# A convolutional feed-forward block's first pass: every sum on VectorE, two weight operands split at once, two pairs side by side

## The chip, the cores and the metric

The kernel runs on one core of a Trainium2 chip. The metric is the device time of one execution in microseconds, as the median over runs. Five engines work in order, each through its own queue, and wait for each other by semaphores: TensorE (PE in the profile; its weight loads are PEld), VectorE (DVE), ScalarE (ACT), GpSimd (POOL), and SyncE (SP), which here issues nearly all DMA transfers.

## The reference

One layer of a bidirectional encoder over 2304 positions (a request of 2048 and one of 256, with the same weights), model width 1024, feed-forward width 2816. The mixers come first (an mLSTM and a grouped attention); the change touches only what follows:

```
x = x + concat(m_out, a_out) @ w_out
h = rmsnorm(x, norm2_w)
u = centred_dwconv(h @ w_up, conv_w, conv_b)      # width 3 over positions
a, g = split(u, 2)                                # 2816 channels each
y = x + (silu(g) * a) @ w_down
out = rmsnorm(y, final_norm_w)
```

All data are float32.

## The kernel before

**Stages.** The program runs the input projection and the mixers, then the output projection with the second norm (`phase_c`, lines 893 to 975, matmuls at L932), then the **first pass** of the feed-forward (`up_phase`: `h @ w_up`, convolution, gate), then the second pass (`down_phase`, matmuls at L1311). Before the code of the first pass is reached, `body` begins it inside `phase_c`: it forms the first block's operand sums, loads three operands and starts one pair.

**Seven products for eight.** A product with operands cut 2 by 2 is done with seven block products and some sums of blocks. Positions are cut in three blocks `b` of 772, 768 and 764 columns, each in two halves of 386, 384 and 382. Seven stationary-side operands come from `w_up` and seven moving ones from `h`; they are named `11`, `21`, `22` (blocks as they are) and `t1` to `t4` (sums). Float32 operands are split in a high part, rounded to fp32r by ScalarE (L1050 for weights, L1007 for `h`), and the rest, by a VectorE subtraction (L1051, L1008); each product takes three matmuls (hi·hi, hi·lo, lo·hi) for each of 4 chunks of 128, so 12 matmuls in a row.

**A pair** is two neighbouring rows of 128 channels (`jj`, `jj + 1`) of `w_up`; it takes the seven products, 84 matmuls, into three PSUM banks `pa`, `pb`, `pc`. Between products ScalarE copies `pa` or `pc` out to tiles `u` (L1101) and VectorE adds (L1104); `pa` and `pc` go on accumulating after such a copy, so the next product into the bank waits for it. Each **turn** `gi` (0 to 10) of a block has two pairs, the gate's and then the value's. The pairs' PSUM tiles lie by turns in two pools of four banks. In `up_start` a pair loads its weights (`ru`), does products `11` and `21`; in block 0 its four weight sums are formed on GpSimd (`w_sums`, L1039) and stored to DRAM (`wsu_d`), from where blocks 1 and 2 load them; the returned `rest` does the other five.

**After a pair.** `conv` does the centre tap on ScalarE (L1173) and two taps on VectorE (L1180, 768 columns each); `silu` is on ScalarE; VectorE multiplies gate and value (L1223); GpSimd forms the sums for the second pass (L1196); all is stored to `act_d`. Turns 3 to 6 of blocks 0 and 1 also form the next block's operand sums on GpSimd (`n2_sums`, L1027), and every turn of block 1 forms sums of `w_down` (`w_sums` again) for the second pass. `n2_block` loads and splits the next block's seven operands.

**What sets the order.** The code is written to the queues by a scheduler that lays out the instructions of each engine ahead of time from its own times; tile pools with a number of buffers (`RW` for raw weights, `WU` for split ones, `UB` for `u`, `TMB` for sums) decide which load has to wait for which release. On the chip each queue is followed strictly in that order.

Of the kernel before, what the change touches and what calls it, by code (L numbers as in the profile page):

```python
# [37 lines left out]
NB = T // BT  # L38
NTB = 8
CX = 8  # L40
WU = 6
NX0 = 2
NPC = 1
WSTEP = 2
# [20 lines left out]
LEAD = 1.3  # L65
WD = 4
YB = 4
UB = 3
RW = 5
PO = 4  # L70
PB = 4
PEB = 3
# [959 lines left out]
def w_sums(g, s1, a11, a12, a21, a22, dst, nm):  # L1032


    nc = g.nc
    t1, t2, t4 = (s1.tile([P, D // 2], F32, tag="tmp", name=f"tw{k}_{nm}", bufs=TMB) for k in (1, 2, 4))
    for k, o, p, q, op in ((2, t1, a21, a22, ALU.add), (0, t2, t1, a11, ALU.subtract),
                           (1, a21, a11, a21, ALU.subtract), (3, t4, a12, t2, ALU.subtract)):
        nc.gpsimd.tensor_tensor(o, p, q, op)  # L1039
        g.st.dma_start(dst[:, k], o)  # L1040
    return {"t1": t1, "t2": t2, "t3": a21, "22": t4}


def split_w(g, s1, src, nm):


    nc = g.nc
    w = s1.tile([P, 2, NCC // 2, P], F32R, tag="wu", name="wu" + nm, bufs=WU)
    hi, lo = (w[:, a].rearrange("p c n -> p (c n)") for a in range(2))
    nc.scalar.activation(hi, src, AF.Copy)  # L1050
    nc.vector.tensor_tensor(lo, src, f32(hi), ALU.subtract)  # L1051
    return w


def up_start(g, s1, ps, ops, b, jj):


    nc = g.nc
    n = (DT[b + 1] - DT[b]) // 2
    nm = f"{b}_{jj}"  # L1060
    h = D // 2

    def raw(k):
        return s1.tile([P, D], F32, tag="raw", name=f"ru{k}_{nm}", bufs=RW)
    r1, r2 = raw(1), raw(2)
    nc.sync.dma_start(r1, g.w_up[jj].rearrange("p c n -> p (c n)"))
    wsrc = {"11": r1[:, 0:h], "21": r1[:, h:D], "t4": r2[:, h:D]}
    dst = g.wsu_d[jj // 2]
    if b:
        r3, r4 = raw(3), s1.tile([P, h], F32, tag="tmp", name=f"ru4_{nm}", bufs=TMB)  # L1070
        nc.sync.dma_start(r3, dst[:, 0:2].rearrange("p k n -> p (k n)"))
        nc.sync.dma_start(r2[:, 0:h], dst[:, 2])
        nc.sync.dma_start(r4, dst[:, 3])
        nc.sync.dma_start(r2[:, h:D], g.w_up[jj + 1, :, NCC // 2:NCC].rearrange("p c n -> p (c n)"))
        wsrc.update({"t2": r3[:, 0:h], "t3": r3[:, h:D], "t1": r2[:, 0:h], "22": r4})
    else:
        nc.sync.dma_start(r2, g.w_up[jj + 1].rearrange("p c n -> p (c n)"))

    def bank(k):
        return ps.tile([P, 512], F32, tag="p", name=f"p{k}_{nm}", bufs=PB)[:, 0:n]  # L1080

    def mul(p, k, add=False):

        w = split_w(g, s1, wsrc[k], f"{k}_{nm}")
        for c in range(NCC // 2):
            for i, (aa, bb) in enumerate(((0, 0), (0, 1), (1, 0))):
                nc.tensor.matmul(p, w[:, aa, c, :], ops[k][:, c, bb, 0:n], start=c == 0 and i == 0 and not add,  # L1087
                                 stop=c == NCC // 2 - 1 and i == 2, skip_group_check=add)
    p1, p2 = bank("a"), bank("b")
    mul(p1, "11")  # L1090
    mul(p2, "21")
    if not b:
        wsrc.update(w_sums(g, s1, r1[:, 0:h], r1[:, h:D], r2[:, 0:h], r2[:, h:D], dst, nm))

    def rest(u1, u2):


        u11, u12, u21, u22 = u1[:, 0:n], u1[:, n:2 * n], u2[:, 0:n], u2[:, n:2 * n]

        def copy(o, p):  # L1100
            nc.scalar.activation(o, p, AF.Copy)  # L1101

        def add(o, p, q):
            nc.vector.tensor_tensor(o, p, q, ALU.add)  # L1104
        copy(u11, p1)
        add(u11, p2, u11)
        mul(p1, "t2", True)
        copy(u12, p1)
        p3 = bank("c")
        mul(p3, "t1")  # L1110
        copy(u21, p3)
        mul(p1, "t3", True)
        copy(u22, p1)
        add(u22, u22, u21)
        mul(p3, "22", True)
        add(u12, p3, u12)
        mul(p1, "t4", True)
        copy(u21, p1)
    return rest


def n2_block(g, s1, sl, sa, b):
    ops = {}
    for k, e in zip(OPS, P1):
        ops.update(n2_ops(sa if b == 1 and k in TWICE else s1 if k in EARLY else sl, b, [k]))
        n2_load(g, ops, b, k, engs=e)
    return ops

# [12 lines left out]
def up_phase(g, tc, st, s1, sl, banks, ops, first):  # L1141
# [10 lines left out]
    nc.sync.dma_start(cw, g.conv)  # L1152
    NC = NW - BLK
    carry = sa.tile([P, 2 * NFC, NC], F32, name="carry")
    turn = [0]
    H = BLK // 2

    def up(b, j):

        rest = first.pop() if first else up_start(g, s1, banks[turn[0] % 2], ops, b, j)  # L1160
        turn[0] += 1
        us = [sp.tile([P, NW], F32, tag="u", name=f"u{b}_{j + k}", bufs=UB) for k in range(2)]
        o = NC if b else 1
        nn = DT[b + 1] - DT[b]
        rest(*(u[:, o:o + nn] for u in us))
        return us

    def conv(b, jj, u, y):
# [18 lines left out]
    def act_ops(b, gi, ya):  # L1187
# [5 lines left out]
        b11, b12, b21, b22 = (ya[:, k, z] for k in range(2) for z in range(2))  # L1193
        t1, t2, t3, t4 = (ts[:, k] for k in range(4))
        for o, p, q in ((t1, b12, b11), (t2, b22, t1), (t3, b22, b12), (t4, b21, t2)):
            nc.gpsimd.tensor_tensor(o, p, q, ALU.subtract)  # L1196
        g.st.dma_start(g.act_d[b, 3:7, :, gi].rearrange("k p n -> p k n"), ts)

    for b in range(ND):
        if b:  # L1200
            ops = n2_block(g, s1, sl, sa, b)
        for gi in range(NG):
            j = 2 * gi
            if b < ND - 1 and SG <= gi < SG + NCC // 2:
                n2_sums(g, s1, b + 1, gi - SG)
            if b == 1:
                r = [s1.tile([P, D], F32, tag="raw", name=f"rd{gi}_{k}", bufs=RW) for k in range(2)]
                for k in range(2):
                    nc.sync.dma_start(r[k], g.w_down[0, (j + k) * P:(j + k + 1) * P, :])
                h = D // 2  # L1210
                w_sums(g, s1, r[0][:, 0:h], r[1][:, 0:h], r[0][:, h:D], r[1][:, h:D],
                       g.wsd_d[:, :, gi].rearrange("k p n -> p k n"), f"d{gi}")
            yg = sa.tile([P, 2, 2, H], F32, tag="y", name=f"yg{b}_{j}", bufs=YB)
            ya = sa.tile([P, 2, 2, H], F32, tag="y", name=f"ya{b}_{j}", bufs=YB)
            for y, jj in ((yg, j + NFC), (ya, j)):
                us = up(b, jj)
                for k in range(2):
                    yk = y[:, k].rearrange("p z n -> p (z n)")
                    conv(b, jj + k, us[k], yk)
                    if y is yg:  # L1220
                        nc.scalar.activation(yk, yk, AF.Silu)
                    else:
                        nc.vector.tensor_tensor(yk, yk, yg[:, k].rearrange("p z n -> p (z n)"), ALU.mult)  # L1223
            act_ops(b, gi, ya)


def down_phase(g, tc, st, s1, sl, banks):
# [23 lines left out]
    def wts(b, k, g0, g1):  # L1251
# [83 lines left out]
def body(tc, aps, phases="abcd"):  # L1335
# [5 lines left out]
    with ExitStack() as st:  # L1341
# [70 lines left out]
        with ExitStack() as s2:  # L1412
# [11 lines left out]
            for f in todo:  # L1424
                f()

            first = [up_start(g, s1, pd, ops, 0, NFC)]
            g.c_end()
            s_wo.close()
            phase_d(g, tc, s1, pd, ops, first)  # L1430
# [88 lines left out]
```

## Time and profile before

| | us |
|---|---|
| median of 3 runs | 3448.78 (3447.7 to 3454.29) |
| the profiled execution | 3458.05 |
| its span, first to last instruction | 3456.3 |
| outside the span | 1.75 |
| PE busy, share of the span | 95% |
| DVE busy | 77% |
| ACT busy | 59% |
| POOL busy | 35% |
| mean granted TensorE clock | 0.980 |

The first pass' matmuls begin at 1860 us and end at 2939 us of the span. A row of the groups view reads: line, engine, operation, output tile <- input tiles, shape, count; busy time and mean of one; the idle time of the engine just before, and what ended it. A row of the windows view has a stretch, its length, and then each engine's busy time with its count of instructions, the granted clock, the DMA engines' busy share and GB/s. Durations of neighbouring instructions overlap a little, and a matmul's duration is about twice the distance to the next start.

### The profile page before, as it was taken

Reading aid. Unit: us, or ns where it says so; the run is one execution under the profiler, and the core shown is the slowest. Engines: PE = TensorE matmul, PEld = TensorE weight load, DVE = VectorE, ACT = ScalarE, POOL = GpSimd, SP = SyncE. Lnnn points to the kernel's source line nnn. Section 1 sums busy time; section 2 is a strip of 40 time slices with the busy share of each in tenths; the row PEclk is TensorE's granted clock in tenths of the full one; section 3 lists DMA queues with packets and bytes.
Section 4 is the critical chain, followed back from the end, with each engine's and each line's share of the span. In section 5 each row is a group of like instructions: output and inputs, shape, how many; then the busy total and the mean of one; then the engine's idle time right before and its main releaser. Section 6 shows DMA issues by size and latency. Waiting matters only on the chain.

```text
span 3456.3 us, 56346 instructions
## 1 busy us (share of the span) xinstructions
PE 3299.8 (95%) x19566; PEld 3054.8 (88%) x19566; DVE 2650.3 (77%) x4298; ACT 2047.3 (59%) x4490; POOL 1205.7 (35%) x1370
## 2 busy tenths in 40 slices
PE   7989999999999999999997999998999999999998
PEld 6778888888888888878897989988999999999998
DVE  7875687778767787887754999998998888766664
ACT  4535666666666676665543645565567777655553
POOL 7774023213241332311136676655432111110101
PEclk9999999999999999999998999999999999999999
DMA  7765233233343434432258464577666556967673
GB/s 240 218 187 166 90 118 104 89 115 103 101 126 114 144 117 126 150 116 87 96 177 286 171 218 174 200 249 264 235 242 203 177 173 199 325 222 270 215 237 123
DMA packets 407085, 601.88 MB, mean 174 GB/s; under 512 B 32496, under 2 KB 256784, under 8 KB 406800
## 3 DMA queue, kind: packets, MB, share of 16 engines
q1 hardware_dynamic: 374256, 553.43, 48.8%
q0 software_dynamic: 11088, 33.04, 3.4%
q10 hardware_dynamic: 21456, 11.80, 1.1%
q8 instruction: 154, 2.52, 0.3%
q14 instruction: 131, 1.07, 0.1%
HBM read 434.23 MB, written 163.92 MB: 173 GB/s over the span
## 4 chain that ended last, share of the span: by engine, by line
PE 67%; DVE 11%; issue 7%; POOL 5%; ACT 5%; DMA 5%; SPq 0%; POOLq 0%; DVEq 0%; ACTq 0%
PE pa L1087 11%; PE pf L1311 7%; PE pc L1087 5%; PE po L932 4%; PE ph L1311 4%; PE mv L682 4%; PE mj L672 4%; PE ps L544 3%; PE pv L564 3%; PE ps L545 3%; PE pv L562 3%; PE pv L563 3%; PE px L521 3%; PE pb L1087 2%; PE pg L1311 2%
## 5 line engine op out<-in xcount | busy, mean ns | idle before, releaser
L550 DVE TENSOR_TENSOR xx<-pe,xx 128x512 fp32r<-128x512 f32 x520 | 371.7, 727 | 171.8 <-ACT xx L549 168.6
L1087 PE MATMUL pa<-nt,wut 128*128 128x386 f32 (+2 forms) x2376 | 457.4, 343 | 19.4 <-ACT u L1101 17.5
L1087 PEld LDWEIGHTS pa<-nt,wut 128*128 128x128 f32 x2376 | 427.2, 192 | 24.5 <-ACT u L1101 21.5
L548 ACT ACTIVATE pe<-ps 128x512 f32<-128x512 f32 x520 | 298.6, 595 | 155.6 <-PE ps L545 141.0
L522 DVE TENSOR_REDUCE mx<-px 128x1 f32<-128x512 f32 (+1 forms) x528 | 339.2, 670 | 50.8 <-PE px L521 49.7
L549 ACT ACTIVATE xx<-pe 128x512 fp32r<-128x512 f32 x520 | 316.1, 633 | 4.7
L932 PEld LDWEIGHTS po<-cmx,wo 128*128 128x128 f32 x1728 | 231.3, 190 | 17.9 <-DVE cx L937 0.8
L932 PE MATMUL po<-cmx,wo 128*128 128x256 f32 x1728 | 241.2, 282 | 0.9 <-DVE cx L937 0.6
L1196 POOL TENSOR_TENSOR ts<-ya 128x384 f32<-128x384 f32 x66 | 115.9, 1757 | 350.7 <-DVE ya L1223 347.4
L1051 DVE TENSOR_TENSOR wut<-ru,wut 128x512 fp32r<-128x512 f32 x220 | 224.9, 1023 | 16.9 <-ACT wut L1050 14.2
L564 PE MATMUL pv<-xx,vv 128*128 128x512 f32 x520 | 214.8, 413 | 13.0 <-DVE xx L550 12.8
L544 PE MATMUL ps<-qq,kk 128*128 128x512 f32 x520 | 214.6, 416 | 1.3 <-ACT pe L548 0.6
L562 PE MATMUL pv<-xx,vv 128*128 128x512 f32 x520 | 209.6, 403 | 1.9 <-ACT rs L572 1.1
L545 PE MATMUL ps<-qm,kl 65*128 65x512 f32 x520 | 208.5, 404 | 0.1
L563 PE MATMUL pv<-xx,vl 128*64 128x512 f32 x520 | 206.9, 398 | 0.0
L672 PE MATMUL mj<-mn,wm 128*128 128x256 f32 x1296 | 199.8, 288 | 6.7 <-ACT og L686 4.8
L682 PE MATMUL mv<-wm,mn 128*128 128x256 f32 x1296 | 204.0, 286 | 1.9 <-ACT qb L678 1.9
L672 PEld LDWEIGHTS mj<-mn,wm 128*128 128x128 f32 x1296 | 185.1, 193 | 22.8 <-ACT og L686 5.6
L682 PEld LDWEIGHTS mv<-wm,mn 128*128 128x128 f32 x1296 | 186.5, 190 | 19.0 <-ACT qb L678 2.5
L521 PE MATMUL px<-kk,qq 128*128 128x512 f32 (+1 forms) x528 | 198.0, 407 | 2.9 <-ACT qq L509 1.5
L1087 PE MATMUL pa<-n,wu 128*128 128x386 f32 (+2 forms) x792 | 171.0, 355 | 30.5 <-DVE wu L1051 25.6
L227 PE MATMUL pj<-w_a,n1T 128*128 128x512 f32 (+1 forms) x864 | 181.2, 365 | 11.1 <-DVE n1T L185 7.8
(315 smaller groups left out, 8317.9 us busy)
## 6 DMA issues: line engine op xcount, KB each, us to landing
mn<-n_d SPq DMA_DIRECT2D x216, 256.0 KB, 3.2
ru<-w_up SPq DMA_DIRECT2D x88, 512.0 KB, 3.7
act_d<-ts SPq DMA_DIRECT2D x33, 768.0 KB, 5.0
nt<-act_d SPq DMA_DIRECT2D x60, 384.0 KB, 5.2
re_t<-wsd_d SPq DMA_DIRECT2D x45, 512.0 KB, 5.6
ru<-wsu_d SPq DMA_DIRECT2D x44, 512.0 KB, 5.3
ru<-wsu_d SPq DMA_DIRECT2D x88, 256.0 KB, 4.5
act_d<-ya SPq DMA_DIRECT2D x99, 192.0 KB, 2.1
```

The costliest lines, as they stand in the source:

```text
L522: nc.vector.tensor_reduce(s.mx[:, t, z0:z0 + 1], ps[:, 0:w], AX.X, ALU.max)
L544: nc.tensor.matmul(ps[:, 0:N], kk[:, kc:kc + P], s.qq[:, 0:N], start=True, stop=False)
L545: nc.tensor.matmul(ps[:, 0:N], kl1[:, kc:kc + P], s.qm[:, 0:N], start=False, stop=True)
L549: nc.scalar.activation(x[:, 0, 0:N], pe[:, 0:N], AF.Copy)
L550: nc.vector.tensor_tensor(x[:, 1, 0:N], pe[:, 0:N], f32(x[:, 0, 0:N]), ALU.subtract)
L562: nc.tensor.matmul(s.pv[:, 0:N], vv[:, kt % 4, :], x[:, 0, 0:N], start=kt == 0, stop=False)
L564: nc.tensor.matmul(s.pv[:, 0:N], vv[:, kt % 4, :], x[:, 1, 0:N], start=False, stop=kt == s.nk - 1)
L672: nc.tensor.matmul(pj[:, o], s.w[c][:, a, o * P:(o + 1) * P], nT[c][:, h, :], start=(c + o + k == 0), stop=(c == NCC - 1 and k == 2 and o ...
L682: nc.tensor.matmul(pv[:, o], nT[c][:, a, o * P:(o + 1) * P], s.w[c][:, h, 256:512], start=(c + o + k == 0), stop=(c == NCC - 1 and k == 2 ...
L932: nc.tensor.matmul(po[:, o], wo[c][z // 2][:, a, n], mx[c][:, h, :], start=(c == 0 and k == 0), stop=(c == NCC - 1 and k == 2))
L1087: nc.tensor.matmul(p, w[:, aa, c, :], ops[k][:, c, bb, 0:n], start=c == 0 and i == 0 and not add, stop=c == NCC // 2 - 1 and i == 2, skip_ ...
L1311: nc.tensor.matmul(ps[c], w[:, aa, c, :], t[:, gi - g0, bb, 0:H], start=gi == 0 and m == 0 and not more, stop=gi == NG - 1 and m == 2, ski ...
```

## The change

- All sums of the first pass move from GpSimd to VectorE: the weight sums, the operand sums, the sums of the gated activations, and those halves of the operand splits that GpSimd had.
- `split_w` splits two neighbouring operands (`11` and `21`, `t2` and `t1`, `t3` and `22`) with one ScalarE and one VectorE instruction of 1024 columns; only `t4` is split alone. The weight sums lie in two tiles of 1024, stored with one DMA each (before: four of 512), and the second pass uses the same split.
- The gate's pair and the value's pair run side by side, step by step, each in its own four banks. The next turn's pairs load, split and do products `11` and `21` (`begin`) ahead of the present turn's taps, silu, product and sums (`gate`) in the code.
- Silu and the product of gate and value take 1536 columns at once; two of the four activation sums become one instruction of 768.
- Buffers: raw weights 5 to 4, `u` 3 to 6, split weights 6 single ones to 4 double and 2 single, sums 3 of 512 to 4 of 1024. The second buffers for `11` and `21` of block 1 go. The sums of `w_down` are spread over odd turns of blocks 1 and 2.

```diff
-WU = 6
+WU = {1: 2, 2: 4}
-UB = 3
-RW = 5
+UB = 6
+RW = 4
-P0 = ((V, G),) * 4
-P1 = ((V, G),) * 7
+P0 = ((V, V),) * 4
+P1 = ((V, V),) * 7
...
-def n2_sums(g, pool, b, c, engs=("gpsimd",) * 4):
+def n2_sums(g, pool, b, c, engs=("vector",) * 4):
...
+def w_sums(g, sa, a11, a12, a21, a22, dst, nm):
+    h = D // 2
+    x, y = (sa.tile([P, D], F32, tag="sum", name=f"tw{k}_{nm}", bufs=SMB) for k in range(2))
+    t2, t1, t3, t4 = x[:, 0:h], x[:, h:D], y[:, 0:h], y[:, h:D]
+    for o, p, q, op in ((t1, a21, a22, ALU.add), (t2, t1, a11, ALU.subtract),
+                        (t3, a11, a21, ALU.subtract), (t4, a12, t2, ALU.subtract)):
+        nc.vector.tensor_tensor(o, p, q, op)
+    for k, t in enumerate((x, y)):
+        g.st.dma_start(dst[:, 2 * k:2 * k + 2], t.rearrange("p (k n) -> p k n", k=2))
...
+    def step(s, k, ops, sa, u1, u2):
+        if k == 0:
+            s.w.update(zip(("t2", "t1"), split_w(g, s.s1, s.x, "b" + s.nm)))
+            s.copy(u11, s.p1)
+            s.add(u11, s.p2, u11)
+            s.mul(s.p1, "t2", ops, True)
+        elif k == 1:
+            s.copy(u12, s.p1)
+            s.p3 = s.bank("c")
+            s.mul(s.p3, "t1", ops)
+        elif k == 2:
+            s.w.update(zip(("t3", "22"), split_w(g, s.s1, s.y, "c" + s.nm)))
+            s.copy(u21, s.p3)
+            s.mul(s.p1, "t3", ops, True)
+        elif k == 3:
+            s.copy(u22, s.p1)
+            s.add(u22, u22, u21)
+            s.mul(s.p3, "22", ops, True)
+        elif k == 4:
+            s.w["t4"], = split_w(g, sa, s.a22, "d" + s.nm)
+            s.add(u12, s.p3, u12)
+            s.mul(s.p1, "t4", ops, True)
+        else:
+            s.copy(u21, s.p1)
...
+    for i, (b, gi) in enumerate(seq):
...
+        us = rest(b, gi, prs)
+        if i + 1 < len(seq):
+            nb, ng = seq[i + 1]
+            if nb not in opsb:
+                opsb[nb] = n2_block(g, s1, sl, nb)
+            prs = begin(nb, ng)
+        gate(b, gi, us)
```

**TensorE's queue within block 0.** In the names, `pa_0_28` is the bank `pa` of block 0, row 28 (a gate's pair; rows 22 and up are the gate's); the moving operand stands first behind the arrow. Before, the middle of pair 28, with the begin of pair 6 in between:

```order
L1087 MATMUL pa_0_28_24006<-nt2_0_22418,wut2_0_28_24053 128x386 x12
L1087 MATMUL pc_0_28_24069<-nt1_0_23115,wut1_0_28_24070 128x386 x11
L1087 MATMUL pa_0_6_24149<-n11_0_22416,wu11_0_6_24151 128x386 x2
L1087 MATMUL pa_0_28_24006<-nt3_0_23116,wut3_0_28_24086 128x386 x12
L1087 MATMUL pa_0_6_24149<-n11_0_22416,wu11_0_6_24151 128x386 x9
L1087 MATMUL pc_0_28_24069<-n22_0_23117,wu22_0_28_24103 128x386 x12
L1087 MATMUL pa_0_6_24149<-n11_0_22416,wu11_0_6_24151 128x386
L1087 MATMUL pb_0_6_24150<-n21_0_22417,wu21_0_6_24166 128x386
L1087 MATMUL pa_0_28_24006<-nt4_0_23118,wut4_0_28_24119 128x386 x12
```

Now, a whole turn but its last two products (the gate's pair 30 and the value's pair 8):

```order
L1082 MATMUL pa_0_30_24166<-n11_0_22416,wa0_30_24163 128x386 x12
L1082 MATMUL pa_0_8_24172<-n11_0_22416,wa0_8_24169 128x386 x12
L1082 MATMUL pb_0_30_24197<-n21_0_22417,wa0_30_24163 128x386 x12
L1082 MATMUL pb_0_8_24210<-n21_0_22417,wa0_8_24169 128x386 x12
L1082 MATMUL pa_0_30_24166<-nt2_0_22418,wb0_30_24285 128x386 x12
L1082 MATMUL pa_0_8_24172<-nt2_0_22418,wb0_8_24302 128x386 x12
L1082 MATMUL pc_0_30_24320<-nt1_0_23099,wb0_30_24285 128x386 x12
L1082 MATMUL pc_0_8_24334<-nt1_0_23099,wb0_8_24302 128x386 x12
L1082 MATMUL pa_0_30_24166<-nt3_0_23100,wc0_30_24347 128x386 x12
L1082 MATMUL pa_0_8_24172<-nt3_0_23100,wc0_8_24363 128x386 x12
L1082 MATMUL pc_0_30_24320<-n22_0_23101,wc0_30_24347 128x386 x12
L1082 MATMUL pc_0_8_24334<-n22_0_23101,wc0_8_24363 128x386 x12
```

Between `t2` and `t3`, both into bank `pa`, there stood 13 matmuls before, and between `t3` and `t4` 23; now 36 stand between them, three products of 12.

**VectorE's queue within block 0.** `wu`, `wut`, `wa` to `wd` are split weights, `tw` weight sums, `u` the results, `yg` and `ya` the gate's and the value's taps. Before, single splits of 512 between taps and adds:

```order
L1051 TENSOR_TENSOR wu21_0_30_24330<-ru1_0_30_24309,wu21_0_30_24330 128x512
L1051 TENSOR_TENSOR wut2_0_30_24360<-tw2_0_30_24346,wut2_0_30_24360 128x512
L1104 TENSOR_TENSOR u0_7_24193<-u0_7_24193 128x386
L1051 TENSOR_TENSOR wut1_0_30_24377<-tw1_0_30_24345,wut1_0_30_24377 128x512
L1104 TENSOR_TENSOR u0_6_24192<-pc_0_6_24212,u0_6_24192 128x386
L1051 TENSOR_TENSOR wut3_0_30_24393<-ru2_0_30_24310,wut3_0_30_24393 128x512
```

Now the sums of the next turn (rows 32 and 10) stand there, between the adds of the present one, with one split of 1024:

```order
L1089 TENSOR_TENSOR u0_9_24284<-u0_9_24284 128x386
L1040 TENSOR_TENSOR tw0_0_32_24543<-tw0_0_32_24543,ru1_0_32_24441 128x512
L1089 TENSOR_TENSOR u0_30_24281<-pc_0_30_24320,u0_30_24281 128x386
L1040 TENSOR_TENSOR tw1_0_32_24544<-ru1_0_32_24441,tw0_0_32_24543 128x512
L1040 TENSOR_TENSOR tw0_0_10_24553<-ru2_0_10_24551 128x512
L1040 TENSOR_TENSOR tw1_0_10_24554<-ru1_0_10_24447,ru2_0_10_24551 128x512
L1089 TENSOR_TENSOR u0_8_24283<-pc_0_8_24334,u0_8_24283 128x386
L1055 TENSOR_TENSOR wb0_32_24565<-tw0_0_32_24543,wb0_32_24565 128x2x512
```

The sums moved into this queue, and the split `wb` of the next turn's pair 32 stands behind them, ahead of the present turn's taps.

**SyncE's queue at the start of the pass.** `nt1` to `nt4` and `n22` are the four operands of block 0 that can be loaded only once `phase_c` has given its memory back; `wsu_d` takes the stored weight sums. Before:

```order
L1040 DMA wsu_d_65<-tw1_0_24_23434 128x512
L1040 DMA wsu_d_65<-tw2_0_24_23435 128x512
L1040 DMA wsu_d_65<-ru2_0_24_23399 128x512
L1006 DMA nt1_0_23115<-n2t_d_62 128x2x386 x2
L1006 DMA nt3_0_23116<-n2t_d_62 128x2x386 x2
```

Now:

```order
L951 DMA n2_d_61<-cx8_3_22738 128x2x256
L1042 DMA wsu_d_65<-tw0_0_24_23433 128x1024
L1042 DMA wsu_d_65<-tw1_0_24_23434 128x1024
L1005 DMA nt1_0_23099<-n2t_d_62 128x2x386 x2
L1005 DMA nt3_0_23100<-n2t_d_62 128x2x386 x2
```

In both, the loads stand behind stores of the third pair's weight sums (row 24), which GpSimd formed before and VectorE forms now.

More of the change, by code (lines that the diff above doesn't have):

```diff
@@ L1119, in up_start, with copy, add, sums @@
-    return rest
-def n2_block(g, s1, sl, sa, b):
+                s.nc.tensor.matmul(p, w[:, aa, c, :], ops[k][:, c, bb, 0:s.n], start=c == 0 and i == 0 and not add,
+                                   stop=c == NCC // 2 - 1 and i == 2, skip_group_check=add)
+    def copy(s, o, p):
+        s.nc.scalar.activation(o, p, AF.Copy)
+    def add(s, o, p, q):
+        s.nc.vector.tensor_tensor(o, p, q, ALU.add)
+    def sums(s, sa):
+        g, h, nc = s.g, D // 2, s.nc
+        dst = g.wsu_d[s.jj // 2]
+        if s.b:
+            s.x, s.y = (sa.tile([P, D], F32, tag="sum", name=f"rs{k}_{s.nm}", bufs=SMB) for k in range(2))
+            for k, t in enumerate((s.x, s.y)):
+                nc.sync.dma_start(t, dst[:, 2 * k:2 * k + 2].rearrange("p k n -> p (k n)"))
+            s.a22 = s.raw(2, h)
+            nc.sync.dma_start(s.a22, g.w_up[s.jj + 1, :, NCC // 2:NCC].rearrange("p c n -> p (c n)"))
+        else:
+            r2 = s.raw(2)
+            nc.sync.dma_start(r2, g.w_up[s.jj + 1].rearrange("p c n -> p (c n)"))
+            s.x, s.y = w_sums(g, sa, s.r1[:, 0:h], s.r1[:, h:D], r2[:, 0:h], r2[:, h:D], dst, s.nm)
+            s.a22 = r2[:, h:D]
@@ L1154, in up_phase, with begin, rest @@
     carry = sa.tile([P, 2 * NFC, NC], F32, name="carry")
-    turn = [0]
     H = BLK // 2
[L1158 to L1162, printed above, removed]
+    def begin(b, gi):
+        prs = [UpPair(g, s1, banks[0], b, 2 * gi + NFC)] if not first else [first.pop()]
+        prs.append(UpPair(g, s1, banks[1], b, 2 * gi))
+        for k, p in enumerate(prs):
+            if (b, gi, k) != (0, 0, 0):
+                p.mul(p.p1, "11", opsb[b])
+        for k, p in enumerate(prs):
+            if (b, gi, k) != (0, 0, 0):
+                p.second(opsb[b])
+        return prs
+    def rest(b, gi, prs):
+        for p in prs:
+            p.sums(sa)
         o = NC if b else 1
         nn = DT[b + 1] - DT[b]
-        rest(*(u[:, o:o + nn] for u in us))
+        us = [[sp.tile([P, NW], F32, tag="u", name=f"u{b}_{p.jj + k}", bufs=UB) for k in range(2)] for p in prs]
+        for k in range(6):
+            for p, u in zip(prs, us):
+                p.step(k, opsb[b], sa, *(x[:, o:o + nn] for x in u))
         return us
@@ L1197, in act_ops @@
+        nc.vector.tensor_tensor(ts[:, 3], ya[:, 1, 0], ts[:, 2], ALU.subtract)
         g.st.dma_start(g.act_d[b, 3:7, :, gi].rearrange("k p n -> p k n"), ts)
[L1199 to L1224, printed above, removed]
@@ L1425, in body @@
                 f()
[L1427 removed]
+            first = [UpPair(g, s1, pd, 0, NFC)]
+            first[0].mul(first[0].p1, "11", ops)
+            first[0].second(ops)
             g.c_end()
```

130 lines of the change are left out of this document (58 added, 72 removed).

## The prediction

> **What bounds the kernel now.** I read the windows view first, over the whole span and then over the first pass of the feed-forward: the pass' begin, then its blocks 0, 1 and 2 (columns: stretch, length, busy time and instructions of PE, PEld, DVE, ACT, POOL; granted TensorE clock, DMA share, GB/s).
>
> ```profile
> 1860.00:1900.00 40.00, 23.39 (x103) 21.36 (x102) 21.95 (x27) 17.37 (x27) 27.98 (x18) 0.74 0.90 317
> 1900.00:2250.00 350.00, 327.62 (x1779) 322.61 (x1778) 327.31 (x322) 195.51 (x371) 240.90 (x139) 0.97 0.55 192
> 2250.00:2608.00 358.00, 334.67 (x1842) 327.82 (x1841) 322.03 (x333) 208.44 (x428) 166.51 (x107) 0.98 0.73 248
> 2608.00:2939.00 331.00, 327.18 (x1858) 325.93 (x1858) 276.37 (x342) 235.11 (x515) 69.21 (x49) 0.99 0.56 182
> ```
>
> TensorE is the bound in all four, but it is full only in the last. What the same matmuls cost without a gap is read from starts in the TensorE timeline (12 matmuls of 386 columns, then 12 of 384) and from an undisturbed window of 382 columns:
>
> ```profile
> 1912.04 2.30 PE L1087 MATMUL pb<-n,wu 128*128 128x386 f32 x12
> 1914.17 2.30 PE L1087 MATMUL pc<-n,wu 128*128 128x386 f32 x12
> ...
> 2602.04 2.27 PE L1087 MATMUL pa<-nt,wut 128*128 128x384 f32 x12
> 2604.14 2.27 PE L1087 MATMUL pc<-n,wu 128*128 128x384 f32 x12
> ...
> 2700.00:2800.00 100.00, 100.00 (x574) 100.00 (x573) 81.61 (x104) 69.83 (x155) 18.05 (x13) 1.00 0.53 169
> ```
>
> So 2.13/12 = 0.1775, 2.10/12 = 0.175 and 100/574 = 0.174 us each. Length less count times price gives what each stretch loses: the begin 40 - 89 x 0.1775 - 2 (its 14 other, short matmuls) = 22; block 0 350 - 1779 x 0.1775 = 34; block 1 358 - 1842 x 0.175 = 36; block 2 331 - 1858 x 0.174 = 8. Together **100 us** is all that the pass can give. Who ends the waits, from the waits view of TensorE between 1900 and 2939 us:
>
> ```profile
> PE pa L1087 <- DVE wu L1051: 25.6, 17, 3.6
> PE pa L1087 <- ACT u L1101: 15.8, 11, 2.9
> PE pa L1087 <- ACT wu L1050: 4.8, 3, 2.8
> ```
>
> These three are 46 of the 78 us lost behind the begin. Most of the rest is a slower clock after such waits: (1 - 0.97) x 350 + 0.02 x 358 + 0.01 x 331 = 21 us, so it goes where the waits go. The first is weights that VectorE splits late, and VectorE is late because GpSimd holds it up. Durations (min/median/max, ns) over the pass, of a split, a tap with both tensors in SBUF, the product of gate and value, and of two adds in block 0, the first with one input in PSUM, the second with both in SBUF; then GpSimd's two costliest groups in block 0:
>
> ```profile
> L1051 DVE TENSOR_TENSOR wut<-ru,wut x220: 675/692/2028, 1862.3 to 2926.7; 128x512 fp32r<-128x512 f32 x110
> L1180 DVE SCALAR_TENSOR_TENSOR yg<-u,cw,yg x132: 1002/1019/2290, 1907.1 to 2933.1; 128x768 f32<-128x768 f32 x88, 128x767 f32<-128x767 f32 x44
> L1223 DVE TENSOR_TENSOR ya<-ya,yg x66: 941/950/2047, 1923.5 to 2959.2; 128x768 f32<-128x768 f32 x66
> ...
> L1104 DVE TENSOR_TENSOR u<-pb,u x21: 545/547/549, 1900.1 to 2236.4; 128x386 f32<-128x386 f32 x21
> L1104 DVE TENSOR_TENSOR u<-u x21: 545/562/1698, 1903.2 to 2224.8; 128x386 f32<-128x386 f32 x21
> ...
> L1196 POOL TENSOR_TENSOR ts<-ya 128x384 f32<-128x384 f32 x20 | 51.1, 2555 | 39.2 <-DVE ya L1223 39.2
> L1039 POOL TENSOR_TENSOR tw<-ru,tw 128x512 f32<-128x512 f32 x20 | 36.1, 1807 | 9.6 <-issue 6.9 <-DMA wsu_d<-tw 2.0 <-DVE wu L1051 0.7
> ```
>
> The same instruction takes 0.69 or 2.0 us; an add with one input in PSUM never varies, one with two in SBUF does. That is the sign of a path which two SBUF inputs share with GpSimd.
>
> **Removing the contention, adding the sums.** With GpSimd silent I take VectorE's medians. A split of 1024 isn't in the trace; 512 takes 0.692 and 768 takes 0.950, so 1.0 ns per element more, thus 1.21 for 1024 and 1.72 for the product of 1536. A sum of 512 costs a split's 0.69, one of 384 an add's 0.56. VectorE per turn of block 0: splits 6 x 1.21 + 2 x 0.69 = 8.6; weight sums 8 x 0.69 = 5.5; adds 6 x 0.56 = 3.4; taps 8 x 1.02 = 8.2; product 1.7; activation sums 0.95 + 2 x 0.56 = 2.1. Together 29.5 us of durations, but neighbours overlap:
>
> ```profile
> 2855.72 0.69 DVE L1051 TENSOR_TENSOR wu<-ru,wu 128x512 fp32r<-128x512 f32 x1
> 2856.33 1.77 DVE L1180 SCALAR_TENSOR_TENSOR ya<-u,cw,ya 128x768 f32<-128x768 f32 x1
> ```
>
> The next starts 0.61 us after a split of 0.69. With 0.08 off for 34 instructions it is 26.8 us. TensorE needs 168 x 0.1775 = 29.8 us for a turn. Turns 3 to 6 add four operand sums (about 2.0): 28.8, nearly full. The last turn adds the next block's 14 splits of 772 columns, 12.3 us, but no weight sums for block 1: 33.6. Block 0 is 11 x 26.8 + 8 + 12 - 5 = 310 us of VectorE against 328 of TensorE; block 1 (no weight sums, about five turns with sums of `w_down`) some 265 against 323. ScalarE, 196 to 235 us busy in each block, stays below.
>
> A full VectorE need not stop TensorE if its work is early. I followed the new orders of both through a turn of block 0, T = 0 at its first `11`. The add of the value's third result can't run before product `22` ends, T = 25.6; then come one split, two sums, five taps and two `t4` splits before the split `wb` of the second pair, which ends at T = 35. Its product starts at T = 29.8 + 10.6 = 40.4: 5 us early, and the first pair's `wb` (T = 27.3 against 38.3) 11 us. Through the last turn with the operand splits I find none later than its product either: `t3`'s ends at 31 against 46.8. A copy out of a bank now has 36 matmuls, 6.4 us, before the bank is written again, where 13, 2.3 us, were; so the waits on `u` (15.8) go as well. By this count blocks 0 to 2 lose nothing; bounds are 0 and today's 78. I take **10 us**, near the lower end, since the last of them, with a VectorE busy for 276 of 331 us, loses 8.
>
> **The begin.** Today's idle time has one large piece. Timelines of TensorE, GpSimd and SyncE, and the one VectorE row that stands ahead of the sums now:
>
> ```profile
> 1878.03 2.37 PE L1087 MATMUL pb<-n,wu 128*128 128x386 f32 x12
> 1892.48 5.19 PE L1087 MATMUL pc<-nt,wut 128*128 128x386 f32 x14 [12.08 <-ACT nt L1007]
> ...
> 1881.59 1.70 POOL L1039 TENSOR_TENSOR tw<-ru 128x512 f32<-128x512 f32 x1
> 1883.37 1.26 POOL L1039 TENSOR_TENSOR tw<-tw,ru 128x512 f32<-128x512 f32 x1
> 1884.59 1.26 POOL L1039 TENSOR_TENSOR ru<-ru,ru 128x512 f32<-128x512 f32 x1
> ...
> 1885.88 0.32 SPq L1040 DMA_DIRECT2D wsu_d<-ru  x1
> 1886.29 1.95 SPq L1006 DMA_DIRECT2D nt<-n2t_d  x4
> ...
> 1874.66 3.22 DVE L949 SCALAR_TENSOR_TENSOR cx<-cx,nw,rs_c 128x256 f32<-128x256 f32 x8 [1.16 <-PE rs_c L135]
> ```
>
> Four early loads for block 1 (operands `11` and `21`, with their splits on GpSimd and VectorE) leave this place. The loads of `nt1` stand in SyncE's queue behind the third pair's stored sums, which GpSimd ends at 1885.8. VectorE gets to the last of those sums after about 13 us of sums, splits and short waits from 1862, the norm's eight instructions (3.2 us, so to 1878.5; now they end at 1877.9) and two more sums; so the stores go at 1880.6 and the loads at 1881, 5 us earlier. As now, 6.2 us later, at 1887, the first matmul on `nt1` runs. By then TensorE has done one product more (`t2` of the second pair, 2 us) and idles 5 us where `wb` of the first pair waits behind the sums, and 9 before `nt1`; with 2 for the clock the begin loses **16** instead of 22. Bounds: 8, if `wb` comes in time and the loads a few us earlier still; 25, if VectorE, now in the path of the norm too, is 9 us later.
>
> **Edits at nothing:** one raw buffer fewer, hidden by the early loads (a turn's second load must be in by T = 24.6 and lands at about 22; without that cover each later microsecond eats the 5 us of `wb`); sums of `w_down` in odd turns, where VectorE has 4 us or more to spare; the second pass, which keeps its matmuls and waits.
>
> **Sum:** 100 - 16 - 10 = 74 us off the profiled 3458.05 (span 3456.3 and 1.75 around it), thus 3384. The runs' median, 3448.78, lies 9.3 below that execution; off it, **3375**.
>
> Rule against the change: the Trainium skill, Perfetto Trace Analysis, section Optimizing Scalar/DVE Operations, says that with VectorE saturated, work may be moved to ScalarE or even GpSimd, and adds that the two share a read port so that it might not help. By its first half undoing such a move would lose (third case below); the two add rows above speak for the second half.
>
> **Rivals.** (1) *VectorE becomes the bound in block 0.* Speaks for it: 26.8 to 28.8 of 29.8 us leave no room, each wait of VectorE on an add is lost, and 14 splits come on top at the block's end. If its instructions come out 20% above my count (32.2 us a turn with the waits), each turn of block 0 loses 2.4, the last some 10, block 1 a few: about 40 more, 3415. Against: 5 to 11 us of lead per turn. (2) *Nothing moves:* the waits on splits were of another origin and come back as waits on adds; 3449. Against: block 2, where GpSimd is busy for 69 us only, loses 8. (3) *Slower: VectorE's long durations aren't GpSimd's doing.* Then it keeps today's 327 us in block 0 and gets 88 weight sums (61), 16 operand sums (9) and the activation sums (23), less about 22 by merging: 398 against 350 today; block 1 gets 322 + 15 + 9 + 23 + 12 - 22 = 359 of 358. With the 6 us of the begin, 3449 + 48 + 1 - 6 = 3492. It decides once an instruction with GpSimd silent stays above 0.9 us for 512 columns; the minimum of 0.675 and the lone add row speak against it.
>
> **How the numbers follow.** Forecast 3375 (3360 to 3395): chance 0.63. Rival 1, from 3395 to 3440: 0.22. Rival 2: 0.05. Rival 3 or another loss of the kind: 0.10. Faster by over 0.2% (7 us, what a measurement of this kernel can tell) 0.85, within 0.2% 0.06, slower 0.09. Range: below, all but the begin's lower bound of 8 gone is 3449 - 92 = 3357; above, rival 1 with 50 us lost is 3425. Outside it I leave 2 in 10.
>
> **What would show it.** Right: GpSimd without an instruction between 1890 and the second pass; splits of 1024 at 1.2 us and no VectorE instruction of 512 above 0.8; about 26 us between the last `phase_c` matmul and the first on `nt1`, where 32 are now (1860.6 to 1892.5); TensorE's waits behind it under 15 us in sum, clock 0.99 or 1.00. VectorE 90% or more busy in block 0 is expected and no harm by itself. Wrong: splits still at 2 us (rival 3), or waits of `pa` on `wa` or `wb` in most turns of block 0 (rival 1), or the `nt1` loads issued after 1884.

## The result, and the profile after

The changed kernel takes 3366.91 us (median, 3360.99 to 3374.49) where the kernel before takes 3449.25 beside it (3447.7 to 3454.29): a ratio of 0.976, 95% interval 0.9737 to 0.9783, or 82 us less. 3375 was predicted. The profiled execution takes 3368.61 us (span 3366.9), 89.4 less than the one before. Of these, 87 lie between the end of `phase_c`'s matmuls and the last matmul of the first pass: 1860.4 to 2938.9 us before, 1859.6 to 2850.7 now.

The windows view of the changed kernel, cut as before into begin and blocks 0, 1 and 2:

```profile
1859.60:1899.60 40.00, 29.42 (x145) 27.66 (x144) 33.19 (x47) 17.52 (x25) 3.94 (x3) 0.87 0.88 306
1899.60:2215.00 315.40, 315.40 (x1779) 315.18 (x1778) 292.91 (x374) 194.35 (x306) 0.00 (x0) 1.00 0.62 218
2215.00:2539.00 324.00, 324.00 (x1850) 324.00 (x1849) 276.73 (x338) 208.93 (x358) 0.00 (x0) 1.00 0.70 241
2539.00:2853.00 314.00, 314.00 (x1795) 314.00 (x1794) 265.52 (x314) 216.34 (x416) 0.00 (x0) 1.00 0.65 223
```

In the three blocks TensorE is busy all the time at a clock of 1.00, with VectorE at 293 of 315 us in block 0 and GpSimd without one instruction. Length less count times price, as in the prediction, gives a loss of 14 us in the begin (135 long matmuls, and 2 us for 10 short ones) and of 0, 0 and 2 us in the blocks: 16 in place of 100. All waits of TensorE for other engines in the pass, from its waits view (us in total, times, longest), stand before 1889 us:

```profile
PE pb L1082 <- DVE cx L949: 4.2, 1, 4.2
PE rs_c L129 <- POOL cacc L945: 2.2, 1, 2.2
PE pa L1082 <- DVE wb L1055: 2.1, 1, 2.1
PE pc L1082 <- ACT nt L1006: 1.7, 1, 1.7
PE pc L1082 <- DVE nt L1007: 0.4, 1, 0.4
```

VectorE's durations over the pass (min/median/max, ns; first to last start) have lost their spread. Splits of two operands, single splits, a tap, an add with both inputs in SBUF; then, from the groups of block 0, product and activation sums:

```profile
L1055 DVE TENSOR_TENSOR wa<-ru,wa x66: 1205/1224/1228, 1852.7 to 2810.4; 128x1024 fp32r<-128x1024 f32 x66
L1055 DVE TENSOR_TENSOR wd<-ru,wd x66: 678/684/693, 1861.6 to 2823.0; 128x512 fp32r<-128x512 f32 x66
L1207 DVE SCALAR_TENSOR_TENSOR yg<-u,cw,yg x132: 1003/1011/1019, 1902.3 to 2858.4; 128x768 f32<-128x768 f32 x88, 128x767 f32<-128x767 f32 x44
L1089 DVE TENSOR_TENSOR u<-u x66: 542/558/564, 1898.8 to 2844.4; 128x386 f32<-128x386 f32 x22, 128x384 f32<-128x384 f32 x22, 128x382 f32<-128x382 f32 x22
...
L1221 DVE TENSOR_TENSOR ya<-ya,yg 128x1536 f32<-128x1536 f32 x10 | 17.5, 1749 | 0.0
L1225 DVE TENSOR_TENSOR ts<-ya 128x768 f32<-128x768 f32 x10 | 9.5, 948 | 0.0
```

A gate's tap that took up to 2.29 us takes 1.02 at most, a split of 512 at most 0.69 where it took up to 2.03. What is left of the begin, from the timeline of TensorE, VectorE and SyncE:

```profile
1876.14 3.22 DVE L949 SCALAR_TENSOR_TENSOR cx<-cx,nw,rs_c 128x256 f32<-128x256 f32 x8
1879.50 3.75 PE L1082 MATMUL pb<-n,wa 128*128 128x386 f32 x12 [4.15 <-DVE cx L949]
1881.63 2.63 SPq L1005 DMA_DIRECT2D nt<-n2t_d  x4
1887.12 0.61 PE L1082 MATMUL pc<-nt,wb 128*128 128x386 f32 x2 [1.75 <-ACT nt L1006]
```

The second pair's first product into `pb` waits for the norm's eight instructions (its bank is released by them; they read `rs_c` in PSUM); the loads of `nt1` go at 1881.6, the first matmul on it runs at 1887.1.

### The profile page after: what moved, and what is told of

Its sections match the earlier page's. It is cut to its first block, busy times and chain, and to the rows that moved or that the text cites. A ratio compares the mean times of both kernels' runs of the same rounds, so it can differ in the third digit from the quotient of the medians.

```text
span 3366.9 us, 54718 instructions
## 1 busy us (share of the span) xinstructions
PE 3267.3 (97%) x19566; PEld 3033.5 (90%) x19566; DVE 2561.9 (76%) x4259; ACT 2015.5 (60%) x4154; POOL 686.9 (20%) x1040
## 4 chain that ended last, share of the span: by engine, by line
PE 74%; DVE 7%; issue 5%; DMA 5%; POOL 4%; ACT 4%; SPq 0%; POOLq 0%; ACTq 0%; DVEq 0%
PE pa L1082 16%; PE pc L1082 8%; PE po L932 5%; PE pf L1338 5%; PE pb L1082 4%; PE mj L672 4%; PE mv L682 4%; PE ps L544 3%; PE ps L545 3%; PE pv L564 3%; PE px L521 3%; PE pv L562 3%; PE pv L563 3%; PE pg L1338 2%; PE ph L1338 2%
## 5 line engine op out<-in xcount | busy, mean ns | idle before, releaser
L1296 POOL TENSOR_TENSOR sq<-sq,sq 128x384 f32<-128x384 f32 x38 | 48.8, 1284 | 1394.9 <-ACT sq L1292 1314.6
L1086 ACT ACTIVATE u<-pa 128x386 f32<-128x386 f32 (+2 forms) x264 | 129.2, 490 | 172.1 <-PE pa L1082 171.2
L227 PEld LDWEIGHTS pj<-w_a,n1T 128*128 128x128 f32 x864 | 144.1, 196 | 30.4 <-DVE n1T L185 7.8
L776 ACT ACTIVATE dm<-dm,tm 128x128 f32<-128x128 f32 x288 | 95.7, 392 | 100.4 <-POOL dm L773 95.9
L1082 PE MATMUL pb<-n,wa 128*128 128x386 f32 (+2 forms) x792 | 147.1, 340 | 4.2 <-DVE cx L949 4.2
```

The lines of the kernel that those rows point to most:

```text
L227: nc.tensor.matmul(pjs[t][:, c0:c1], nTs[tiles[t]][:, c, a, :], ws[c][:, b, c0:c1], start=(c == 0 and k == 0), stop=(c == NCC - 1 and k == 2))
L1082: s.nc.tensor.matmul(p, w[:, aa, c, :], ops[k][:, c, bb, 0:s.n], start=c == 0 and i == 0 and not add, stop=c == NCC // 2 - 1 and i == 2, s ...
```

## The experiments

Two theories were set against each other. **A:** the gain is GpSimd's silence; its sums held up VectorE's instructions with two inputs in SBUF. **B:** the gain is the new order, which gives copies and splits more matmuls as cover. The times of a group were taken on one chip beside the kernel before (3454.2, 3452.5 and 3460.7 us in the three groups), so ratios are compared. The scheduler lays out all queues anew for each of these kernels, and a change of engine can change their order too.

### Engine and order apart

First the changed kernel with its sums back on GpSimd:

```diff
-P0 = ((V, V),) * 4
-P1 = ((V, V),) * 7
+P0 = ((V, G),) * 4
+P1 = ((V, G),) * 7
...
-        nc.vector.tensor_tensor(o, p, q, op)
+        nc.gpsimd.tensor_tensor(o, p, q, op)
```

(in `n2_sums` and for the three sums `ts` likewise)

> The changed kernel with all its sums (weights, operands, activations) and half of the operand splits back on GpSimd; order, merged splits, side-by-side pairs kept. Theory A (the gain is GpSimd's silence): before, VectorE's 322 instructions of block 0 held some 101 us beyond their medians, 0.73 us for each of 139 GpSimd instructions. With the same load on GpSimd VectorE would be at 214 + 101 = 315 us of 315 in block 0 and 320 of 324 in block 1: blocks lose 20 to 35 and 15 to 30 us, the begin some 6: 3420 us (3395 to 3445), single splits of 512 again up to 2 us. Theory B (the gain is the new order, with 36 matmuls instead of 13 between two products into a bank): 3367 to 3385, though VectorE's durations grow.

Measured: 3411.49 us, ratio 0.9875 (0.9859 to 0.9891). Then the kernel before with the same edit the other way round, every `nc.gpsimd` of its first pass replaced by `nc.vector`:

> The kernel before with nothing changed but the engine of all its sums and operand splits: VectorE instead of GpSimd. Theory A: VectorE's instructions return to their medians (split 0.69 us, tap 1.02); with single splits a turn of block 0 takes it 27.5 us of 29.8, and with the old order some waits on u stay (15.8 us before): 3400 us (3385 to 3425). Theory B: the sums only add to a VectorE that was already late, and the order is the old one: 3440 or more.

Measured: 3395.93 us, ratio 0.9825 (0.9809 to 0.9842). Both times lie at A's numbers, but neither reaches the changed kernel, so the rest of the change carries a part. Windows of the second run, begin, block 0 up to its end, the change of blocks, block 1 and what follows:

```profile
1860.00:1900.00 40.00, 24.47 (x113) 22.85 (x112) 29.14 (x43) 18.05 (x27) 3.42 (x3) 0.74 0.81 280
...
1900.00:2180.00 280.00, 279.76 (x1577) 278.98 (x1576) 263.33 (x407) 168.30 (x320) 0.00 (x0) 1.00 0.62 207
2180.00:2240.00 60.00, 53.76 (x287) 52.28 (x286) 54.33 (x80) 40.42 (x75) 0.00 (x0) 0.94 0.78 264
2240.00:2500.00 260.00, 251.83 (x1407) 248.59 (x1407) 222.18 (x339) 156.36 (x325) 0.00 (x0) 0.99 0.77 261
```

With the code in its old order and a silent GpSimd, block 0 up to 2180 us loses nothing (280 - 1577 x 0.1775 = 0). What stays is the begin (20 us), the change from block 0 to 1 (60 - 287 x 0.177 = 9) and the middle of block 1 (260 - 1407 x 0.175 = 14), where TensorE waits for ScalarE:

```profile
2217.18 4.23 PE L1087 MATMUL pc<-n,wu 128*128 128x386 f32 x12 [3.85 <-ACT u L1101]
...
2400.92 1.01 PE L1087 MATMUL pa<-n,wu 128*128 128x384 f32 x2 [4.51 <-ACT wu L1050]
```

The first run shows the other half: the new order with GpSimd busy. Block 0 of it, and its splits of two operands:

```profile
1900.00:2235.00 335.00, 324.19 (x1791) 321.73 (x1790) 290.01 (x248) 189.74 (x303) 229.87 (x125) 0.98 0.58 204
...
L1055 DVE TENSOR_TENSOR wa<-ru,wa x66: 1210/2030/2868, 1854.6 to 2851.1; 128x1024 fp32r<-128x1024 f32 x66
```

VectorE has no sums to do there and is as long busy as with all of them (290 us), because its instructions are held up: the split `wa`, 1.22 us in the changed kernel, takes 2.03 in the median. Loss against a full TensorE, in us:

| | begin | block 0 | block 1 | block 2 | sum |
|---|---|---|---|---|---|
| before | 22 | 34 | 36 | 8 | 100 |
| old order, sums on VectorE | 20 | 9 | 15 | 1 | 45 |
| new order, sums on GpSimd | 21 | 17 | 10 | 7 | 55 |
| changed kernel | 14 | 0 | 0 | 2 | 16 |

(Block 0 and 1 of the second row are 325 and 335 us with 1779 and 1831 matmuls, of the third 335 and 335 with 1791 and 1860; block 2 is 323 with 1849 and 321 with 1803.) The change of engine in the old code is worth 1.75% (60 us), the rest of the change without it 1.25% (43 us), both 2.4% (82): each takes in part the same waits. The first isn't the engine's doing alone, for the queues moved with it. Between 1920 and 2180 us the kernel before has its products `t2`, `t3` and `t4` singly in TensorE's queue, 12 matmuls each; with the sums on VectorE two of them follow each other 14 times, 24 on end. What this is worth no run shows. In the new order TensorE's products in block 0 follow each other alike with the sums on either engine, and there the engine is worth 2.4 less 1.25%, some 40 us.

### The contention by itself

Three runs add ten GpSimd instructions of 512 columns to every turn of the changed kernel, behind the store of the activation sums and on that tile, which the store is done with by then:

```diff
         g.st.dma_start(g.act_d[b, 3:7, :, gi].rearrange("k p n -> p k n"), ts)
+        tf = ts.rearrange("p k n -> p (k n)")
+        for _ in range(10):
+            nc.gpsimd.tensor_tensor(tf[:, 0:512], tf[:, 512:1024], tf[:, 1024:1536], ALU.subtract)
```

In the second the line is `nc.gpsimd.memset(tf[:, 0:512], 0.0)`, in the third `nc.gpsimd.tensor_copy(tf[:, 0:512], tf[:, 512:1024])`.

> The changed kernel plus, in each of the 33 turns, ten GpSimd tensor_tensor of 512 columns with two inputs in SBUF, on a tile that is otherwise done with (the stored activation sums are overwritten: nothing reads them again). Theory A: each costs VectorE some 0.73 us, 80 us per block: VectorE 373 of 315 us in block 0, 357 of 324 in block 1, 345 of 314 in block 2: some 120 us slower than the changed kernel, 3490 (3440 to 3540). Theory B: VectorE's lead covers it, 3367 to 3390.

> As the run with ten GpSimd tensor_tensor per turn, at the same place and on the same tile, but memsets of 512 columns, which write to SBUF and read nothing. Theory A in its narrow form (what is shared is the path on which two inputs are read): VectorE's durations stay at their medians, 3367 to 3375. If any GpSimd work in SBUF holds VectorE up: well over 3400, with taps and splits above their medians.

> As the runs with ten GpSimd tensor_tensor (3595.6 us) and ten GpSimd memsets (3370.9) per turn, at the same place and on the same tile, but copies of 512 columns, with one input in SBUF. If GpSimd's reading as such holds VectorE up: a copy lasts between a memset (0.53) and a tensor_tensor (1.87 here), and each holds VectorE for about as long as it runs, 0.5 to 0.9 us: 330 times that is 165 to 300 us, of which VectorE's idle 118 us in the three blocks take a part: 3420 to 3560. If it takes two GpSimd inputs: taps and splits at their medians, 3367 to 3376.

Measured: 3595.58 us with two inputs (1.0407, 1.0391 to 1.0422), 3370.86 with none (0.9753, 0.9731 to 0.9775: the changed kernel's own ratio), 3438.15 with one (0.9931, 0.9907 to 0.9954). The added instructions (duration of one, min/median/max) and the value's taps beside them, in this order of runs:

```profile
L1231 POOL TENSOR_TENSOR ts<-ts x330: 1267/1886/3228, 1933.3 to 3114.8; 128x512 f32<-128x512 f32 x165
L1207 DVE SCALAR_TENSOR_TENSOR ya<-u,cw,ya x132: 1002/1932/2055, 1905.4 to 3085.7; 128x768 f32<-128x768 f32 x88, 128x767 f32<-128x767 f32 x44
L1089 DVE TENSOR_TENSOR u<-pb,u x66: 540/547/562, 1867.1 to 3036.3; 128x386 f32<-128x386 f32 x22, 128x384 f32<-128x384 f32 x22, 128x382 f32<-128x382 f32 x22
```

```profile
L1231 POOL MEMSET ts<- x330: 524/527/538, 1938.6 to 2891.9; 128x512 f32 x165
L1207 DVE SCALAR_TENSOR_TENSOR ya<-u,cw,ya x132: 1007/1014/1022, 1910.6 to 2873.1; 128x768 f32<-128x768 f32 x88, 128x767 f32<-128x767 f32 x44
```

```profile
L1231 POOL COPY ts<-ts x330: 614/1221/9231, 1938.8 to 2959.7; 128x512 f32<-128x512 f32 x165
L1207 DVE SCALAR_TENSOR_TENSOR ya<-u,cw,ya x132: 1001/1358/1368, 1911.1 to 2902.9; 128x768 f32<-128x768 f32 x88, 128x767 f32<-128x767 f32 x44
```

330 memsets, 174 us of GpSimd, leave a tap at 1.01 us. Copies, with one input, take it to 1.36 and two inputs to 1.93. An add with one input in PSUM stays at 0.55 beside the worst of them. So it is GpSimd's reading of SBUF against VectorE's second input there. The Trainium skill states this (SBUF — State Buffer, section Who interferes with whom): a VectorE instruction with two inputs in SBUF contends with a GpSimd instruction that reads SBUF, and not with one that only writes it. These three runs agree with it.

The size of the first was missed, 3490 expected. In block 0 (1900 to 2250 us) VectorE's instructions lasted 83 us beyond their medians in the changed kernel, for the 84 GpSimd instructions that fall there: 1.0 us for each, not 0.73. TensorE then waited 141 us in 49 waits behind the begin, and the slower clock after them (0.93 to 0.95 in the blocks) took some 70 more, together about what the blocks lost (207 by length less count times price). In the third row one wait of 3.7 us lies in the begin, and 3.7 us of waits on ScalarE's half of `wb` aren't shown:

```profile
PE pa L1082 <- ACT u L1086: 57.5, 20, 8.2
PE pa L1082 <- DVE wc L1055: 51.5, 23, 6.5
PE pa L1082 <- DVE wb L1055: 32.2, 5, 10.2
```

In blocks 1 and 2 of this run VectorE also waited 17.6 us for GpSimd to be done with the only `ts` tile; block 0 has no such wait.

The time with copies isn't a clean price. In block 0 they held VectorE about 22 us for 80 copies, 0.28 us each. But of the 70 us by which its span (3437.8) exceeds the changed kernel's in a second execution (3368.2, on another chip; by the ratios it is some 58), 46 are one wait of TensorE at the pass' end, where VectorE waited twice for the last copies on the only `ts` tile and the second pass' first weights stood behind. So the range of 3420 to 3560 was met by luck: a hold of 0.5 to 0.9 us was expected, and without this wait the time would lie near 3392. The waits:

```profile
2934.10 0.96 DVE L1225 TENSOR_TENSOR ts<-ya 128x768 f32<-128x768 f32 x1 [10.81 <-POOL ts L1231]
2946.66 0.96 DVE L1225 TENSOR_TENSOR ts<-ya 128x768 f32<-128x768 f32 x1 [10.42 <-POOL ts L1231]
2960.97 1.29 DVE L1055 TENSOR_TENSOR we<-re,we 128x512 fp32r<-128x512 f32 x2 [12.17 <-ACT we L1054]
```

A small dose was tried too, the activation sums alone on GpSimd (`nc.gpsimd` for the three sums `ts`):

> The changed kernel with only the three activation sums of a turn on GpSimd, 99 instructions in the pass. VectorE gets 1.9 us per turn back (20.5 us in block 0) and is held 0.95 us by each of three (what ten per turn cost it, 83 us for 88 instructions in block 0): 1 us more per turn, which still fits into 28.7: 3367 to 3378. If any sum of this size on GpSimd costs time by making single instructions late: 3385 and up.

Measured: 3378.87 us beside 3460.74, ratio 0.9763 (0.9738 to 0.9787), the changed kernel's. TensorE's waits behind the begin come to 4 us. On GpSimd the sum of 768 columns takes 1.86 us in the median and up to 9.6 (3.33 in the mean), against 0.95 on VectorE. In block 0 VectorE's instructions last 21 us longer beside the 30 activation sums that fall there (0.69 us each, 0.95 expected). On VectorE those sums took 20.5 us, so nothing is won either:

```profile
L1225 POOL TENSOR_TENSOR ts<-ya 128x768 f32<-128x768 f32 x33 | 109.8, 3328 | 796.1 <-DVE ya L1221 653.6 <-DMA wsd_d<-tw_d 78.0 <-DMA re<-w_down 28.1
```

### Parts of the order

Each with sums on VectorE first. Splits one by one into the same double tiles:

```diff
-    nc.scalar.activation(hi, src, AF.Copy)
-    nc.vector.tensor_tensor(lo, src, f32(hi), ALU.subtract)
+    for i in range(m):
+        nc.scalar.activation(hi[:, i], src[:, i], AF.Copy)
+        nc.vector.tensor_tensor(lo[:, i], src[:, i], f32(hi[:, i]), ALU.subtract)
```

> The changed kernel with each split of two operands done as two of 512 on ScalarE and on VectorE, into the same double buffers. Theory A: two splits of 512 start 0.61 us apart, so a pair of them takes VectorE 1.22 us, as long as one of 1024 (1.22): 3367 to 3373, no change. Theory C (the merged splits are what makes VectorE fit): a fixed cost of at least 0.1 us times 6 a turn on each engine shows as waits of products on split weights in block 0, 10 us or more: 3377 and up.

Measured: 3372.62 us beside 3452.54, ratio 0.9768 (0.9747 to 0.979). The changed kernel, run again in the same group:

> The changed kernel as it is, timed beside the others on the same chip: 3361 to 3374.

Measured: 3372.42, ratio 0.9767 (0.9747 to 0.9786). Merging two splits is worth nothing here. Next the pairs one after the other in the code:

```diff
-        for k in range(6):
-            for p, u in zip(prs, us):
+        for p, u in zip(prs, us):
+            for k in range(6):
...
                 p.mul(p.p1, "11", opsb[b])
-        for k, p in enumerate(prs):
-            if (b, gi, k) != (0, 0, 0):
                 p.second(opsb[b])
```

> The changed kernel with the gate's five steps first and then the value's, and products 11 and 21 of a pair together, so that two products into one bank stand 12 matmuls apart (2.1 us) instead of 36, unless the scheduler mixes them; sums stay on VectorE. Theory A alone (only VectorE's speed matters): 3367 to 3375. Theory B (the order that gives copies and adds time carries part of the gain): waits of TensorE on u return, 15.8 us of them before, plus the slower clock after them: 3385 to 3405.

Measured: 3375.92, ratio 0.9776 (0.9759 to 0.9793), a microsecond above A's range and not told apart from the changed kernel; no wait of TensorE on a `u` in the blocks. The scheduler mixes the two pairs here as well, with some 24 matmuls between products into one bank in place of 36, so this edit takes away only a third of the cover. Each of these edits again, now with the sums on GpSimd, where VectorE is late:

> The changed kernel with both edits: pairs one after the other and all sums back on GpSimd (alone they gave 3375.9 and 3411.5 us). If putting the pairs side by side is the part of the order that takes waits away while VectorE is late: waits of TensorE on u and split weights grow, 3425 to 3450. If it does nothing: 3408 to 3420.

> The changed kernel with both edits: splits of 512 and all sums back on GpSimd (alone 3372.6 and 3411.5 us). If fewer, longer VectorE instructions meet fewer of GpSimd's (splits of 1024 were held 45 us in block 0 beyond 1.22 us each, splits of 512 in the kernel before 62 beyond 0.69): some 20 us more of VectorE in block 0, 3420 to 3440. If merging does nothing here either: 3408 to 3418.

Measured: 3436.54 us for the pairs (0.993, 0.9907 to 0.9954) and 3424.85 for the splits (0.9896, 0.9872 to 0.9919), beside 0.9875 (0.9859 to 0.9891) with neither edit. The pairs cost 0.55%, 19 us, and their waits are those on the copies; first this run's row, then that of the new order with sums on GpSimd:

```profile
PE pa L1082 <- ACT u L1086: 33.8, 14, 5.5
```

```profile
PE pa L1082 <- ACT u L1086: 10.1, 7, 3.6
```

For the splits the intervals overlap: a cost of some 7 us by the ratios, not shown. (The 3424.85 lies in the first range, but the chip of this group is 0.2% slower.) The one trace has 33 us of TensorE's waits behind the begin, 20 of them on `wc`, where there were 19 with neither edit, so a small cost is likely.

### The begin

Here the sums of the second turn's first two pairs wait for the norm (by a copied column), and their stores leave SyncE's queue:

```diff
+        g.cx = x
...
+    if nm in ("0_24", "0_2"):
+        for t in (x[:, h:h + 1], y[:, 0:1]):
+            nc.vector.tensor_copy(t, g.cx[3][:, 1, 0:1])
...
-        g.st.dma_start(dst[:, 2 * k:2 * k + 2], ...
+        (nc.gpsimd if nm in ("0_24", "0_2") else g.st).dma_start(dst[:, 2 * k:2 * k + 2], ...
```

> The changed kernel with the sums of the second turn's first two pairs made to wait for the norm's last eight VectorE instructions (by a copy of one column each), and with their stores on GpSimd's queue, so that the loads of nt1 stand right behind the norm's stores in SyncE's queue. If the begin is bound by this chain (norm at 1876.1, loads at 1881.6, first matmul on nt1 at 1887.1): the norm starts near 1873, the loads go near 1878, the first matmul on nt1 near 1883: 3 to 5 us faster than the changed kernel, 3362 to 3364. If the begin is bound by the sums and splits on VectorE in any order: the same within 2 us, or slower by up to 3.

Measured: 3372.1 us, ratio 0.9763 (0.9748 to 0.9778), the same as the changed kernel's 0.9767 beside it. From its timeline:

```profile
1874.26 3.22 DVE L949 SCALAR_TENSOR_TENSOR cx<-cx,nw,rs_c 128x256 f32<-128x256 f32 x8 [0.44 <-PE rs_c L135]
...
1884.20 0.61 PE L1086 MATMUL pc<-nt,wb 128*128 128x386 f32 x2 [2.09 <-ACT nt L1007]
...
1889.74 0.85 ACT L1007 ACTIVATE nt<-nt 128x772 fp32r<-128x772 f32 x1 [4.62 <-DMA nt<-n2t_d]
...
1894.26 0.45 PE L1086 MATMUL pa<-nt,wc 128*128 128x386 f32 x1 [1.47 <-ACT nt L1007]
```

The norm runs 1.9 us earlier and the first matmul on `nt1` 2.9, each about 1.2 us short of what was expected (1873 and 1883). The gain is given back 10 us later: the first half of `nt3` reaches ScalarE at 1889.7, and TensorE waits for the second until 1894.3. The DMA engines are 0.85 busy in these 40 us (0.88 in the changed kernel), and the begin loses 17 us here, 16 in the changed kernel of the same group. Whether fewer bytes in this stretch would shorten it wasn't tried.

## Why the prediction was right

- **The bound and the 100 us:** right. 84 of the 100 went, all of it in the first pass.
- **VectorE at its medians:** right, and by the mechanism that the two add rows suggested. 1.22 us for a split of 1024 (1.21 expected), 1.75 for the product (1.72), 0.95 for the sum of 768. The window of block 0 takes VectorE 293 us. The 310 expected were for all 1848 matmuls of the block; for the window's 1779 that is 298. VectorE is early: its waits are now for TensorE's products and ScalarE's halves.
- **Blocks, 10 us:** 2 lost. The lower bound was the true one. The argument for 10, that block 2 with a VectorE busy for 276 of 331 us lost 8, took for VectorE's load what was GpSimd's 69 us in that block: with the code in the old order and GpSimd silent it lost 1.
- **The waits on `u`,** put down to 36 matmuls where 13 were: only half shown. With VectorE on time some 24 matmuls serve as well; with VectorE late the cover is worth 19 us. With the code in the old order and sums on VectorE 7.6 us of such waits are left (5.0 on `pc`, 2.6 on `pa`), where 15.8 on `pa` and 0.5 on `pc` were.
- **What the prediction had not counted:** the code in its old order loses 23 us at the change of blocks and in block 1 even beside a silent GpSimd. It put these with the waits that VectorE causes. They went with the rest of the change. Which of its parts took them, the earlier begin, the spread sums of `w_down` or the buffers, no run tells apart.
- **The begin, 16 us:** 14 in this execution, 16 in the second one; `nt1` at 1881.6 and 1887.1 (1881 and 1887 expected), 27.3 us after the last `phase_c` matmul (26). That arrival sets the sum, and it was right; the places of the idle time were not. The 5 us put to `wb` of the first pair were 2 and the 9 put before `nt1` 1.8. Instead 4 stood at the bank `pb` and 2 at the norm's `rs_c`, which weren't foreseen, and some 4 are the slower clock (0.87 in the begin) where 2 were put.
- **The rivals:** VectorE becoming the bound did not happen in block 0 (no wait of TensorE there). Nothing moving, and a loss because VectorE's long durations aren't GpSimd's doing, are refuted by the durations and by the three runs with ten instructions.
- **The offset:** between the two profiled executions the sum was 15 us short (89 against 74), by medians 8 (82). The 9.3 us by which the profiled execution before lay above its median came back as 1.7 after, and hid the half of it: that the forecast of 3375 is only 8 us off is in part luck.

## What to carry to other kernels

If the same VectorE instruction has two durations in a trace, look whether both its inputs lie in SBUF and what GpSimd reads at that time; beside a VectorE that works from SBUF nearly all the time, a GpSimd `tensor_tensor` of 512 columns cost it 1.0 us here, more than the 0.68 in which VectorE does the same sum. Each GpSimd instruction cost it about 0.73 us in block 0 of the kernel before (101 us for 139), and each activation sum 0.69, so having such sums on GpSimd unloaded VectorE by nothing. Work for GpSimd beside a busy VectorE is best without SBUF inputs: its memsets cost nothing. Cover between products (side-by-side pairs) paid where the engine behind was late, and cost nothing measurable where it wasn't.

## What the runs showed of the hardware

The hold has sizes: a GpSimd instruction of 512 columns costs a neighbouring VectorE instruction with two SBUF inputs nothing (memset, 0.527 us), 0.35 us a time (copy: taps at 1.36 for 1.01), or about 0.9 to 1.05 us (two inputs: 1.93 to 2.06). The sizes hardly spread: of 264 taps beside the copies 118 last about 1.35 us, one 1.25 and all others 1.0. GpSimd is held in turn: its copy takes 0.61 us at the least, 1.22 in the median and once 9.2, its `tensor_tensor` 1.27, 1.89 and at most 3.2.
